# Two-layer hybrid decoder: wider weight ring, whole-row splits and five pair slots in the feed-forward parts

## The chip, the cores and the metric

The kernel runs on one core of one Trainium2 chip. A core has five engines with a queue each: TensorE (PE in the profile; its weight loads are a row of their own, PEld), VectorE (DVE), ScalarE (ACT), GpSimd (POOL) and SyncE (SP). On-chip memory is SBUF; matmuls accumulate in the banks of PSUM. The metric is the device time of one execution in microseconds, as the median of several runs. One of the executions is profiled, and its trace tells when each instruction ran.

## The reference

Two layers on a sequence of 256 tokens with 2048 features, all in float32. What matters here is the feed-forward part at the end of each layer, with w1 of 2048 x 8192 and w2 of 8192 x 2048:

```python
def squared_relu_mlp(h, w1, w2):
    z = jax.nn.relu(h @ w1)
    return (z * z) @ w2

for i in range(DEPTH):          # 2
    ...
    x = x + jnp.concatenate([token_out, mem_out], axis=-1) @ w_out[i]
    x = x + squared_relu_mlp(rms_norm(x, ffn_norm[i]), w_ff1[i], w_ff2[i])
```

The rest (a pooling mixer, two kinds of attention, projections) has weights of the same sort, which come through the same feed.

## The kernel before

**Splits.** A float32 operand goes into TensorE as two float32r parts: high = the value cast by ScalarE (`_split`, L179), low = value minus high, by VectorE (L182). A product takes three matmuls: high by high, low by high, high by low. So each weight is loaded, cast and subtracted before TensorE can use it. The class `Feed` does that for all weights in the order of use.

**Feed.** The host lays weights out as rows of 128 x 1024 in the order of use. There are two kinds of work on them. An N job (`quad`) uses 512 columns, half a plain row, as four blocks of 128 x 128. An S job belongs to a slab, two rows that hold a 2 x 2 arrangement of blocks of w2: by Strassen's scheme its seven products take sums of blocks as weights, and four S jobs serve them (j = 0 the first row, 1024 columns; 1 the sum `t1` of two blocks that a DMA accumulated, 512 columns; 2 the second row, 1024; 3 the first row again after VectorE has overwritten it with two sums, the step K, L205 and L207). A first pass of the program over dummies (`dry`) lists the jobs in a `Plan`; `close` makes the list of pieces to prepare.

**Ring.** The high and low parts lie in two rings, `hi_ring` and `lo_ring`, of SLOTS = 6 slots of 512 columns. `_slots` gives the next one or two neighbouring slots in turn, and goes back to the first where two don't fit before the end; where they are still in use the preparation stops and is tried again at the next job. `fill(job)` prepares pieces up to AHEAD = 3 places behind the job in the list; `free` gives a job's slots back. `load` issues the DMAs some loads further ahead (`loads_ahead`, 3, in most of the feed-forward part 4): plain rows and slab rows on SyncE's queue, the accumulating ones on GpSimd's. Four buffers hold plain rows (tile `raw`), three slab rows (tag `rows`, tile `slab`), and the second row of every second slab lies in a part of `room` (`feed.spare`).

The order of instructions on an engine is made by the framework from this program order and the data's dependencies; an instruction that is ready earlier may come ahead of one that stands before it in the program.

**Feed-forward part** (`ffn`, called once a layer). 64 tiles of 128 columns of w1 (`up_tile`), 16 blocks or four N jobs each, by `a_part` (L429 with the high parts for 512 columns, L431 with the low parts for 256), accumulate in one bank, `x_bank`. ScalarE copies the bank out (L812), VectorE adds its halves (L821), ScalarE squares (L827, L829). Two tiles make a pair: `convert` forms the sums that Strassen's scheme needs (L785 to L790), `high` casts them (L795) and `low` subtracts (L799) into one of six pair slots, four in `z` and two in `z_more` (tile `zb`). A pair's slot must be free (`pair_free`) before `high` is put in.

S jobs are put between the quads: `due` takes them from a list by a time, in tiles, that `tiles_at` gives each slab, at least two at the start of a tile, more after its fourth, eighth and twelfth block. Their matmuls are L865, L867 and L868 into seven banks `p`. The seven banks serve the left and the right half of the output in turns of four slabs: `swap` copies a bank to a kept buffer (L924) and the other half's sum back (L916), fourteen copies a turn. The buffers for that are `keep`: seven in `room` and two tiles of the tags `acc2` and `rowsq`. `close_left` sums the left half when it is done, `turn_left` transposes it; `evict` copies a bank into one of two buffers `outs`. Eight more tiles of w2 (`down_tile`, two N jobs each) end the part, between the last eight S jobs.

Of the kernel before, what the change touches and what calls it, by code (L numbers as in the profile page):

```python
# [17 lines left out]
P = 128  # L18
# [37 lines left out]
class Plan:  # L56
# [7 lines left out]
    def __init__(self):  # L64
        self.entries = []
        self.npos = 0
        self.jobs = []
        self.slabs = []

    def close(self):  # L70
        prep = []
        for job in self.jobs:

            prep.append(job)
            if job[0] == "S" and job[2] == 1:
                prep.append(("K", job[1]))
        self.prep = prep
        self.where = {job: i for i, job in enumerate(prep)}
        self.loads = []
        self.need = {}  # L80
        for p in prep:
            if p[0] == "S" and p[2] == 0:
                self.loads += [("S", p[1], 0), ("S", p[1], 1)]
            elif p[0] == "N" and p[1] % 2 == 0:
# [14 lines left out]
class Feed:  # L99


    def __init__(self, tc, wst, wpool, rows, plan, dry):
# [13 lines left out]
        if not dry:  # L116
            self.hi = wpool.tile([P, SLOTS * 512], F32R, name="hi_ring")
            self.lo = wpool.tile([P, SLOTS * 512], F32R, name="lo_ring")
            self.busy = [False] * SLOTS
            self.at = 0  # L120

# [43 lines left out]
    def _slots(self, n):  # L165
        a = self.at if self.at + n <= SLOTS else 0
        if any(self.busy[a : a + n]):
            return None
        for i in range(a, a + n):
            self.busy[i] = True  # L170
        self.at = (a + n) % SLOTS
        return a

    def _split(self, job, src, n):
        a = self._slots(n)
        if a is None:
            return False
        hi, lo = self.hi[:, a * 512 : (a + n) * 512], self.lo[:, a * 512 : (a + n) * 512]
# [9 lines left out]
        self.split[job] = (hi, lo, range(a, a + n))  # L188
        return True

    def _prepare(self, p):
        add = self.nc.vector.tensor_add
        self.load(self.plan.need[p] + 1 + self.loads_ahead)
        if p[0] == "N":
# [38 lines left out]
    def quad(self, what):  # L233

        job = ("N", self.pos // 4)
        if self.dry:
            self.plan.entries += what if isinstance(what, list) else [what]
            if self.pos % 4 == 0:
                self.plan.jobs.append(job)
            return Nothing(), Nothing()  # L240
# [24 lines left out]
    def job(self, n, j):  # L265
        job = ("S", n, j)
        if self.dry:
            self.plan.jobs.append(job)
            return Nothing(), Nothing()
# [18 lines left out]
def program(ctx, tc, plan, dry, xT, memT, par, lam, cst, wst, yT):  # L288
# [437 lines left out]
    def ffn(l, xs, tags, done):  # L726
# [9 lines left out]
        z_more = sp.tile([P, 2, 2, 1024], F32R, tag="big", name=f"zb{l}")  # L736
        staged = sp.tile([P, 2, 1024], F32, tag="big2", name=f"stage{l}")
        outs = [room[:, 512 * j : 512 * j + 512] for j in range(2)]
        feed.t1 = [room[:, 1024 + 512 * j : 1536 + 512 * j] for j in range(3)]
        two_y = room[:, 2560:3584].rearrange("p (a c) -> p a c", a=2)  # L740
        feed.spare = room[:, 3584:4608]
        keep = [room[:, 4608 + 512 * j : 5120 + 512 * j] for j in range(7)]
        for tag in ("acc2", "rowsq"):
            keep.append(tp.tile([P, 512], F32, tag=tag, bufs=1, name="keep"))
        r = []
        banks = []
        cnt = [0]
        done_pairs = set()
        pair_free = [True] * 6
        S1, S3, S2, S4, A12, A22, A11, A21 = range(8)  # L750

        def pair(i):
            i = i % 6
# [875 lines left out]
```

## Time and profile before

| | us |
|---|---|
| median of 3 runs | 2024.43 |
| lowest and highest run | 2023.85, 2027.73 |
| profiled execution | 2022.72 |
| its span | 2021.0 |

The granted TensorE clock was 1.0 throughout. The tiles 4 to 63 of the two feed-forward parts lie about 270 to 900 us and 1350 to 1985 us from the span's start. The loads:

```
raw<-in_w SPq DMA_DIRECT2D x484, 512.0 KB, 4.7
slab<-in_w SPq DMA_DIRECT2D x180, 512.0 KB, 5.3
room<-in_w POOLq DMA_DIRECT2D x180, 256.0 KB, 6.9
```

These are tile and source, queue, count, KB of each and the median us from issue to landing.

How to read the rest: a row of instructions has line, engine, operation, what is written and read (out<-in), shapes and count, then busy us and mean ns of one, then the engine's idle time before them and what ended it. A row of waits has the engine and tile that waited, whom it waited for, total us, times, longest us. Matmuls are pipelined: the one of 512 columns is listed with some 0.39 us, and the next begins 0.23 us after it. A wait shorter than the rest of the matmul before it shows no idle time of PE.

### The profile page before, as it was taken

What the parts mean: (1) busy time and instruction counts of PE and PEld (TensorE: products, weight loads), DVE (VectorE), ACT (ScalarE), POOL (GpSimd) and SP (SyncE); (2) the same over time, 40 slices, a digit from 0 to 9 for tenths busy, and PEclk for the clock granted to TensorE, in tenths of its full rate; (3) what the DMA queues carried; (4) which work ended last, traced back from release to release, by engine and by line L of the source; (5) the groups of instructions that cost most, each with busy time, mean ns of one, the idle gap of its engine ahead of it and who ended that gap; (6) DMA issues with size and microseconds to landing.
All of it is one profiled execution on the core that took longest, in us unless ns stands there. A gap on an engine that the chain in (4) does not pass through costs nothing.

```text
span 2021.0 us, 31924 instructions
## 1 busy us (share of the span) xinstructions
PE 2000.6 (99%) x10510; PEld 1694.8 (84%) x10510; DVE 1701.0 (84%) x2842; ACT 1486.9 (74%) x2582; POOL 260.5 (13%) x307
## 2 busy tenths in 40 slices
PE   9999999999999999999999999999999999999999
PEld 8888888888888888888888888888888888888887
DVE  8888878888888888989765698878888888888898
ACT  7765577687787878878665699567686877878875
POOL 0001211111111111110000000321111111111110
PEclk9999999999999999999999999999999999999999
DMA  8566588999999999975566534578899999999994
GB/s 320 168 204 189 189 252 242 284 266 281 276 271 288 273 266 275 265 231 176 184 233 194 171 126 149 196 211 262 261 274 269 282 278 279 272 283 272 269 275 142
DMA packets 162310, 485.11 MB, mean 240 GB/s; under 512 B 18272, under 2 KB 20960, under 8 KB 162144
## 3 DMA queue, kind: packets, MB, share of 16 engines
q1 hardware_dynamic: 127440, 420.14, 61.0%
q0 software_dynamic: 34560, 62.93, 18.4%
q8 instruction: 82, 1.34, 0.3%
q14 instruction: 84, 0.69, 0.1%
q10 hardware_dynamic: 144, 0.01, 0.0%
HBM read 480.91 MB, written 2.10 MB: 239 GB/s over the span
## 4 chain that ended last, share of the span: by engine, by line
PE 90%; ACT 5%; DVE 3%; issue 1%; DMA 1%; DVEq 0%; ACTq 0%; POOLq 0%
PE x_bank L429 20%; PE x_bank L431 10%; PE p L868 8%; PE p L865 8%; PE p L867 8%; PE wo L429 6%; PE wo L431 3%; ACT hi_ring L179 2%; PE u L429 2%; DVE lo_ring L182 1%; PE ff L429 1%; PE u L431 1%; PE q L463 1%; PE q L465 1%; PE q L464 1%
## 5 line engine op out<-in xcount | busy, mean ns | idle before, releaser
L179 ACT CAST hi_ring<-raw 128x512 fp32r<-128x512 f32 x969 | 590.9, 621 | 260.7 <-DVE lo_ring L182 58.9
L182 DVE TENSOR_TENSOR lo_ring<-raw,hi_ring 128x512 fp32r<-128x512 f32 x969 | 661.9, 697 | 114.9 <-ACT hi_ring L179 100.5
L429 PE MATMUL x_bank<-fx,hi_ring 128*128 128x512 f32 x1952 | 611.2, 394 | 1.2 <-ACT hi_ring L179 1.2
L182 DVE TENSOR_TENSOR lo_ring<-slab,hi_ring 128x1024 fp32r<-128x1024 f32 x300 | 365.5, 1223 | 123.8 <-ACT hi_ring L179 120.5
L431 PEld LDWEIGHTS x_bank<-fx,lo_ring 128*128 128x128 f32 x1952 | 365.8, 188 | 89.8 <-DVE lo_ring L182 6.9
L179 ACT CAST hi_ring<-slab 128x1024 fp32r<-128x1024 f32 x300 | 313.5, 1052 | 141.7 <-PE x_bank L429 64.8
L431 PE MATMUL x_bank<-fx,lo_ring 128*128 128x256 f32 x1952 | 384.6, 278 | 3.4 <-DVE lo_ring L182 3.4
L429 PEld LDWEIGHTS x_bank<-fx,hi_ring 128*128 128x128 f32 x1952 | 320.8, 189 | 28.9 <-ACT hi_ring L179 2.1
L865 PE MATMUL p<-hi_ring,z 128*128 128x512 f32 x588 | 231.8, 394 | 2.8 <-ACT hi_ring L179 2.5
L867 PE MATMUL p<-hi_ring,z 128*128 128x512 f32 x588 | 229.9, 391 | 0.0
L868 PE MATMUL p<-lo_ring,z 128*128 128x512 f32 x588 | 227.6, 393 | 0.4 <-DVE lo_ring L182 0.4
L154 POOL DMA_DIRECT2D room<-in_w x120 | 104.5, 876 | 580.3 <-DMA room<-in_w 564.6
L179 ACT CAST hi_ring<-room 128x512 fp32r<-128x512 f32 x180 | 137.7, 767 | 36.7 <-PE p L867 21.0
L429 PE MATMUL wo<-cat,hi_ring 128*128 128x512 f32 x512 | 161.8, 397 | 0.3 <-DVE rc L400 0.3
L182 DVE TENSOR_TENSOR lo_ring<-room,hi_ring 128x512 fp32r<-128x512 f32 x180 | 155.5, 864 | 6.6 <-ACT hi_ring L179 6.4
L144 POOL DMA_DIRECT2D slab<-in_w x60 | 51.9, 865 | 783.8 <-DVE mm_max L652 352.6
L868 PEld LDWEIGHTS p<-lo_ring,z 128*128 128x128 f32 x588 | 110.0, 188 | 29.6 <-DVE lo_ring L182 6.6
L865 PEld LDWEIGHTS p<-hi_ring,z 128*128 128x128 f32 x588 | 110.3, 188 | 20.4 <-ACT hi_ring L179 6.4
L867 PEld LDWEIGHTS p<-hi_ring,z 128*128 128x128 f32 x588 | 110.5, 188 | 13.7
L431 PEld LDWEIGHTS wo<-cat,lo_ring 128*128 128x128 f32 x512 | 95.9, 188 | 22.0
L868 PE MATMUL p<-lo_ring,zb 128*128 128x512 f32 x252 | 99.7, 396 | 2.0 <-DVE lo_ring L182 1.9
L431 PE MATMUL wo<-cat,lo_ring 128*128 128x256 f32 x512 | 101.5, 279 | 0.0
(382 smaller groups left out, 3270.8 us busy)
## 6 DMA issues: line engine op xcount, KB each, us to landing
raw<-in_w SPq DMA_DIRECT2D x484, 512.0 KB, 4.7
slab<-in_w SPq DMA_DIRECT2D x180, 512.0 KB, 5.3
room<-in_w POOLq DMA_DIRECT2D x180, 256.0 KB, 6.9
room<-in_w SPq DMA_DIRECT2D x120, 256.0 KB, 5.0
room<-in_w SPq DMA_DIRECT2D x60, 512.0 KB, 5.1
slab<-in_w POOLq DMA_DIRECT2D x60, 256.0 KB, 6.0
memraw<-in_mem SPq DMA_DIRECT2D x5, 512.0 KB, 4.2
resid<-in_x SPq DMA_DIRECT2D x8, 256.0 KB, 5.4
```

The costliest lines, as they stand in the source:

```text
L144: self.nc.gpsimd.dma_start(t[:, 0:512], self.wst[h, :, 512:1024], accum_op=ALU.add)
L154: self.nc.gpsimd.dma_start(self.t1[i], right, accum_op=ALU.add)
L179: self.last_cast = self.nc.scalar.copy(hi, src)
L182: low = self.nc.vector.tensor_sub(lo, src, hi.bitcast(F32))
L429: nc.tensor.matmul(ps, hi, xs[:, k, :], start=first and c == 0, stop=False)
L431: nc.tensor.matmul(ps[:, T : 2 * T], lo, xs[:, k, 0:T], start=False, stop=last and c == len(ks) - 1,)
L463: nc.tensor.matmul(ps[t], x[t][1], hi, start=k == 0, stop=False)
L464: nc.tensor.matmul(ps[t], x[t][0], hi, start=False, stop=False)
L465: nc.tensor.matmul(ps[t], x[t][0], lo, start=False, stop=k == NK - 1)
L865: nc.tensor.matmul(ps, a[1], hi, start=new, stop=False, **again)
L867: nc.tensor.matmul(ps, a[0], hi, start=False, stop=False, **again)
L868: nc.tensor.matmul(ps, a[0], lo, start=False, stop=end, **again)
```

## The change

`SLOTS` stays 6, and three more slots are used while a feed-forward part is on (`feed.more`): two in the half of `z_more` that the sixth pair slot had, for wide pieces, and one in two tiles of the tags `acc2` and `rowsq`, for the S job of 512 columns alone. `_slots` now takes any free place of the fitting size, beginning with the next, and pieces of two slots begin at even slots. In a feed-forward part a plain row's two N jobs are one piece, D: one cast and one subtraction over 1024 columns; its slots are given back one by one, as each quad is used, and `where` puts both quads at D's place in the list. Pair slots go from six to five. The two buffers `outs` are gone: `evict` and the last tiles go through the list `keep`, whose nine buffers all lie in `room`.

```diff
@@ -66,22 +66,29 @@
         self.npos = 0
         self.jobs = []
         self.slabs = []
+        self.wide = set()
 
     def close(self):
         prep = []
+        self.where = {}
         for job in self.jobs:
-
+            if job[0] == "N" and job[1] % 2 == 0 and {job, ("N", job[1] + 1)} <= self.wide:
+                self.where[job] = self.where["N", job[1] + 1] = len(prep)
+                prep.append(("D", job[1]))
+                continue
+            if job in self.where:
+                continue
+            self.where[job] = len(prep)
             prep.append(job)
             if job[0] == "S" and job[2] == 1:
                 prep.append(("K", job[1]))
         self.prep = prep
-        self.where = {job: i for i, job in enumerate(prep)}
         self.loads = []
         self.need = {}
         for p in prep:
             if p[0] == "S" and p[2] == 0:
                 self.loads += [("S", p[1], 0), ("S", p[1], 1)]
-            elif p[0] == "N" and p[1] % 2 == 0:
+            elif p[0] in "ND" and p[1] % 2 == 0:
                 self.loads.append(("N", p[1] // 2))
             self.need[p] = len(self.loads) - 1
         rows = sorted(self.loads, key=lambda r: r[0] == "N" and 8 * r[1] + 8 > self.npos)
@@ -116,8 +123,10 @@
         if not dry:
             self.hi = wpool.tile([P, SLOTS * 512], F32R, name="hi_ring")
             self.lo = wpool.tile([P, SLOTS * 512], F32R, name="lo_ring")
-            self.busy = [False] * SLOTS
+            self.busy = [False] * (SLOTS + 3)
             self.at = 0
+            self.more = None
+        self.in_ffn = False
 
     def load(self, upto):
         while self.lp < min(upto, len(self.plan.loads)):
@@ -162,20 +171,31 @@
             ),
         )
 
-    def _slots(self, n):
-        a = self.at if self.at + n <= SLOTS else 0
-        if any(self.busy[a : a + n]):
+    def _slots(self, job, n):
+        ext = job in self.plan.wide and self.more is not None
+        if job[0] == "S" and n == 1 and ext:
+            places = [SLOTS + 2]
+        else:
+            last = SLOTS + 2 if ext and n == 2 else SLOTS
+            first = (self.at + n - 1) // n * n
+            places = [(first + i) % last for i in range(0, last, n)]
+        free = [a for a in places if not any(self.busy[a : a + n])]
+        if not free:
             return None
+        a = free[0]
         for i in range(a, a + n):
             self.busy[i] = True
-        self.at = (a + n) % SLOTS
-        return a
+        if a < SLOTS + 2:
+            self.at = a + n
+        if a < SLOTS:
+            return range(a, a + n), [x[:, a * 512 : (a + n) * 512] for x in (self.hi, self.lo)]
+        return range(a, a + n), self.more[0] if n == 2 else self.more[1]
 
     def _split(self, job, src, n):
-        a = self._slots(n)
-        if a is None:
+        got = self._slots(job, n)
+        if got is None:
             return False
-        hi, lo = self.hi[:, a * 512 : (a + n) * 512], self.lo[:, a * 512 : (a + n) * 512]
+        slots, (hi, lo) = got
         self.last_cast = self.nc.scalar.copy(hi, src)
         if self.cast_behind:
             self.order(self.last_cast, self.cast_behind.pop())
@@ -185,12 +205,22 @@
         if self.behind:
             self.order(low, self.behind)
             self.behind = None
-        self.split[job] = (hi, lo, range(a, a + n))
+        self.split[job] = (hi, lo, slots)
         return True
 
     def _prepare(self, p):
         add = self.nc.vector.tensor_add
         self.load(self.plan.need[p] + 1 + self.loads_ahead)
+        if p[0] == "D":
+            r = ("N", p[1] // 2)
+            one, two = ("N", p[1]), ("N", p[1] + 1)
+            if not self._split(one, self.raw[r], 2):
+                return False
+            del self.raw[r]
+            hi, lo, (a, b) = self.split[one]
+            for job, s, c in ((one, a, 0), (two, b, 512)):
+                self.split[job] = (hi[:, c : c + 512], lo[:, c : c + 512], (s,))
+            return True
         if p[0] == "N":
             r = ("N", p[1] // 2)
             c = p[1] % 2 * 512
@@ -237,6 +267,8 @@
             self.plan.entries += what if isinstance(what, list) else [what]
             if self.pos % 4 == 0:
                 self.plan.jobs.append(job)
+                if self.in_ffn:
+                    self.plan.wide.add(job)
             return Nothing(), Nothing()
         if self.pos % 4 == 0:
             self.fill(job)
@@ -266,6 +298,7 @@
         job = ("S", n, j)
         if self.dry:
             self.plan.jobs.append(job)
+            self.plan.wide.add(job)
             return Nothing(), Nothing()
         self.fill(job)
         return self.split[job][:2]
@@ -734,24 +767,23 @@
         z = sp.tile([P, 4, 2, 1024], F32R, tag=tags[0], name=f"z{l}")
         room = sp.tile([P, 8192], F32, tag=tags[1], name=f"room{l}")
         z_more = sp.tile([P, 2, 2, 1024], F32R, tag="big", name=f"zb{l}")
+        one_more = [tp.tile([P, 512], F32R, tag=t, bufs=1, name="t1_" + t) for t in ("acc2", "rowsq")]
+        feed.more = ([z_more[:, 1, e, :] for e in range(2)], one_more)
+        feed.in_ffn = True
         staged = sp.tile([P, 2, 1024], F32, tag="big2", name=f"stage{l}")
-        outs = [room[:, 512 * j : 512 * j + 512] for j in range(2)]
-        feed.t1 = [room[:, 1024 + 512 * j : 1536 + 512 * j] for j in range(3)]
-        two_y = room[:, 2560:3584].rearrange("p (a c) -> p a c", a=2)
-        feed.spare = room[:, 3584:4608]
-        keep = [room[:, 4608 + 512 * j : 5120 + 512 * j] for j in range(7)]
-        for tag in ("acc2", "rowsq"):
-            keep.append(tp.tile([P, 512], F32, tag=tag, bufs=1, name="keep"))
+        feed.t1 = [room[:, 512 * j : 512 * j + 512] for j in range(3)]
+        two_y = room[:, 1536:2560].rearrange("p (a c) -> p a c", a=2)
+        feed.spare = room[:, 2560:3584]
+        keep = [room[:, 3584 + 512 * j : 4096 + 512 * j] for j in range(9)]
         r = []
         banks = []
-        cnt = [0]
         done_pairs = set()
-        pair_free = [True] * 6
+        pair_free = [True] * 5
         S1, S3, S2, S4, A12, A22, A11, A21 = range(8)
 
         def pair(i):
-            i = i % 6
-            return z[:, i] if i < 4 else z_more[:, i - 4]
+            i = i % 5
+            return z[:, i] if i < 4 else z_more[:, 0]
 
         class Chunks:
 
@@ -764,9 +796,13 @@
                     return half
                 return half[:, 0 if c.start == 0 else 1, :]
 
+        def free_tile():
+            x = keep.pop(0)
+            keep.append(x)
+            return x
+
         def evict(ps):
-            x = outs[cnt[0] % 2]
-            cnt[0] += 1
+            x = free_tile()
             nc.scalar.copy(x, ps)
             return x
 
@@ -788,10 +824,10 @@
                 )
                 nc.vector.tensor_sub(block(S2), block(S1), block(A11))
                 nc.vector.tensor_add(block(S4), block(A12), block(S2))
-                at(1, lambda: when(lambda: pair_free[i % 6], high))
+                at(1, lambda: when(lambda: pair_free[i % 5], high))
 
             def high():
-                pair_free[i % 6] = False
+                pair_free[i % 5] = False
                 nc.scalar.copy(pair(i)[:, 0, 0:n], u[:, 0:n])
                 at(1, low)
 
@@ -836,7 +872,7 @@
             assert all(k // 2 in done_pairs for k in ks)
             if n >= 3:
                 c_tile(ps, "w_ff2", l, n, ks, Chunks())
-                x = outs[cnt[0] % 2]
+                x = free_tile()
                 nc.vector.tensor_mul(x[:, 0:T], ps[:, 0:T], r[0])
                 nc.vector.tensor_add(resid[:, n, :], resid[:, n, :], x[:, 0:T])
                 done(n)
@@ -896,7 +932,7 @@
                     product(p, g, end, side(a), hi[:, s], lo[:, s])
                 feed.job_used(n, j)
                 if j == 3 and not again and i < 28:
-                    pair_free[i % 6] = True
+                    pair_free[i % 5] = True
 
             return run
 
@@ -1073,6 +1109,8 @@
                     tick()
                 if n == 2:
                     finish_banks()
+                if n == 7:
+                    feed.in_ffn, feed.more = False, None
                 down_tile(n, bank() if n < 3 else mmt("ff2"))
 
         return last
```

## The prediction

> **What bounds the kernel now.** First the page of the profile, its busy times:
>
> ```profile
> span 2021.0 us, 31924 instructions
> PE 2000.6 (99%) x10510; PEld 1694.8 (84%) x10510; DVE 1701.0 (84%) x2842; ACT 1486.9 (74%) x2582; POOL 260.5 (13%) x307
> ```
>
> TensorE is busy 99% of the span, so all that any change outside it can win are the moments in which it waits. The list of waits tells for whom (total us, times, longest). The tiles `x_bank` and `p` exist in the two feed-forward parts alone, so these rows are theirs:
>
> ```profile
> PEld p L868 <- DVE lo_ring L182: 14.6, 37, 1.0
> ...
> PEld p L865 <- ACT hi_ring L179: 8.9, 22, 0.8
> ...
> PE x_bank L431 <- DVE lo_ring L182: 3.4, 4, 1.3
> ...
> PE p L865 <- ACT hi_ring L179: 3.3, 8, 0.6
> ...
> PE x_bank L429 <- DVE z L799: 2.3, 2, 1.2
> PE p L868 <- DVE lo_ring L182: 2.3, 5, 0.6
> ...
> PE x_bank L429 <- ACT hi_ring L179: 1.2, 2, 0.6
> ```
>
> Four of the PE rows are waits for a weight piece whose high part (ScalarE, L179) or low part (VectorE, L182) was not ready: 3.4 + 3.3 + 2.3 + 1.2 = 10.2 us of idle TensorE in 19 waits. The one for L799 is the end of each part, where the last pair is converted; the diff doesn't touch that chain. The two PEld rows show that the weight loader waits more often, mostly under a running matmul.
>
> One such wait in the timeline (start, duration, engine, line):
>
> ```profile
> 415.04 0.59 ACT L924 COPY keep<-p 128x512 f32<-128x512 f32 x1
> ...
> 415.51 0.61 ACT L924 COPY room<-p 128x512 f32<-128x512 f32 x1
> ...
> 415.99 1.13 ACT L916 COPY p<-room 128x512 f32<-128x512 f32 x2
> ...
> 417.03 2.02 ACT L179 CAST hi_ring<-slab 128x1024 fp32r<-128x1024 f32 x2
> ...
> 418.13 2.36 DVE L182 TENSOR_TENSOR lo_ring<-slab,hi_ring 128x1024 fp32r<-128x1024 f32 x2 [2.17 <-ACT hi_ring L179]
> ...
> 418.37 0.40 PE L865 MATMUL p<-hi_ring,z 128*128 128x512 f32 x1
> 418.60 0.40 PE L867 MATMUL p<-hi_ring,z 128*128 128x512 f32 x1
> ...
> 419.41 0.50 PE L868 MATMUL p<-lo_ring,z 128*128 128x512 f32 x1 [0.41 <-DVE lo_ring L182]
> 419.74 0.40 PE L865 MATMUL p<-hi_ring,z 128*128 128x512 f32 x1
> ```
>
> ScalarE is exchanging the banks' sums (copies out, L924, and back, L916), so the cast of the slab begins at 417.03, its low part follows at 418.13, and TensorE, there at 418.60 and due on at 418.83, goes on at 419.41. What a wait costs is read here: the step 418.60 to 419.41 is 0.81 us where 418.37 to 418.60 is 0.23, so 0.58 are lost though the row says 0.41, and the next step (0.33) loses another 0.10. A wait costs its idle time plus 0.27 us.
>
> Outside these bursts ScalarE has time, and what holds it is the ring:
>
> ```profile
> ACT hi_ring L179 <- PE x_bank L429: 135.4, 179, 2.5
> ...
> ACT hi_ring L179 <- PE p L867: 73.0, 86, 2.5
> ...
> ACT hi_ring L179 <- DMA raw<-in_w: 6.8, 5, 2.4
> ```
>
> and on SyncE's queue:
>
> ```profile
> SPq L135 <- DVE lo_ring L182: 677.4, 384, 9.5
> ```
>
> 208.4 us it stands before a cast because TensorE has not yet let go of the slot, and 6.8 us for a load. The loads wait for buffers (677.4 us on SyncE's queue) and not buffers for loads. So the waits of TensorE come from too short a lead of the splits against bursts on ScalarE, and the lead is set by the slots.
>
> **The change part by part.**
>
> The order of the matmuls, their number and the DMAs (number and bytes) stay. Removed, added and moved are splits and buffers:
>
> *Rows split whole.* A plain row (1024 columns, two quads) has one cast and one subtraction in place of two each.
>
> ```profile
> L179 ACT CAST hi_ring<-raw 128x512 fp32r<-128x512 f32 x969 | 590.9, 621 | 260.7 <-DVE lo_ring L182 58.9
> L182 DVE TENSOR_TENSOR lo_ring<-raw,hi_ring 128x512 fp32r<-128x512 f32 x969 | 661.9, 697 | 114.9 <-ACT hi_ring L179 100.5
> ...
> L182 DVE TENSOR_TENSOR lo_ring<-slab,hi_ring 128x1024 fp32r<-128x1024 f32 x300 | 365.5, 1223 | 123.8 <-ACT hi_ring L179 120.5
> ...
> L179 ACT CAST hi_ring<-slab 128x1024 fp32r<-128x1024 f32 x300 | 313.5, 1052 | 141.7 <-PE x_bank L429 64.8
> ```
>
> The trace has the wide forms on slabs: 1052 ns for 2 x 621 and 1223 for 2 x 697. A part has 64 tiles of two rows and seven of the last eight tiles of one, 135 rows, 270 in both: ScalarE loses 270 x 190 ns = 51 us of work, VectorE 270 x 171 ns = 46 us. Off the path of TensorE: counted as 0 by itself. The price is latency: the first quad is whole after 1.05 + 1.22 = 2.27 us in place of 0.62 + 0.70 = 1.32, so 0.95 later if the cast begins at the same moment. The cover is the lead worked out below; without it, this is the second rival. A raw row is let go by one subtraction rather than the second of two, so its next load is not later; SyncE's order of issue is the order of the splits' loads as before.
>
> *Ring.* Before, six slots of 512 columns taken in turn, with waste at the wrap; a tile's usual order is S S N N S N S N (S a slab job, N a quad), 2+2+1+1+2+1+2+1 slots. After, four places of two slots, and a place of its own for the one narrow S job of four. The jobs' lengths, at a tile's start:
>
> ```profile
> 420.92 0.65 ACT L179 CAST hi_ring<-raw 128x512 fp32r<-128x512 f32 x1
> ...
> 421.82 0.40 PE L865 MATMUL p<-hi_ring,zb 128*128 128x512 f32 x1
> ...
> 422.02 0.59 ACT L812 COPY room<-x_bank 128x512 f32<-128x512 f32 x1
> ...
> 422.50 0.62 ACT L179 CAST hi_ring<-raw 128x512 fp32r<-128x512 f32 x1
> ...
> 423.19 0.39 PE L865 MATMUL p<-hi_ring,zb 128*128 128x512 f32 x1
> ...
> 423.87 0.61 PE L429 MATMUL x_bank<-fx,hi_ring 128*128 128x512 f32 x2
> ...
> 424.32 0.40 PE L431 MATMUL x_bank<-fx,lo_ring 128*128 128x256 f32 x2
> ...
> 425.25 0.63 PE L429 MATMUL x_bank<-fx,hi_ring 128*128 128x512 f32 x2
> ```
>
> A wide S takes 423.19 - 421.82 = 1.37 us, the narrow one 0.68, an N 425.25 - 423.87 = 1.38. Going through a part's order of jobs with the old rule and the new one, adding these lengths from the job that frees the slot to the job that uses it: before, some 4 of 10 wide S pieces have 2.75 us (one N, one S) or less, the median is 3.5, quads lie between 2.7 and 4.8. After, nearly all S pieces have 4.8 us or more (median 6.2), and rows 5 us or more, but for about 12 of 125 in a part that have 2.7. So the lead grows by some 2 us where it was shortest, and 0.95 of that goes into the latency of the rows; the slabs keep all of it. The waits to be covered are 0.1 to 1.3 us. What bounds it from both sides: nothing is won if the lead isn't used; and all 19 waits are won, 10.2 + 19 x 0.27 = 15.3 us, with perhaps 3 more from loader waits that delay a matmul by a tenth and show as no idle time (18). I take 12: two of the 19, the longest (1.3 us, one in each part, where the left half's banks are closed and VectorE sums them), come from VectorE's queue rather than from slots, and I leave them: 15.3 - 2 x (1.3 + 0.27) = 12.2.
>
> *Five pair slots.* Pair i is written about tile 2i + 3 and needs pair i-5 to be used up. By the slabs' due times the tightest are pairs 9 (pair 4 is free at tile 20.96, wanted at 21), 13 (28.6 against 29) and 5 (12.4 against 13). Nothing is delayed: 0. If one were, the copy L795 would wait on ScalarE for one job (1.4 us), casts queued behind it, and the pair itself is wanted by slabs several tiles later; with some six tight places in two parts at most 6 x 1.4 us of a lead of 5 us, so still 0 on TensorE.
>
> *Eviction buffers.* `evict` and the last tiles take from the nine kept buffers, all now in `room`. While sums are out, two are free, as many as before. No instruction more or less: 0, and the wait for an older reader is the same.
>
> **Sum.** The profiled execution took 2022.72 us, 1.7 around the span of 2021.0. 2022.7 - 12.2 = 2010.5. The median of the three runs, 2024.43, lies 1.7 above the profiled one, so the forecast for a median is 2024.4 - 12.2 = 2012.2, said as 2012.
>
> **The rivals.**
>
> *The three-ahead rule binds, not the slots.* A job still prepares only three pieces ahead, the sums of a slab (K) count as one, and a row counts as one though it serves two jobs, so its second quad prepares nothing. At the start of a tile a row is then put in only two S jobs (2.05 to 2.74 us) ahead. Against it: the cast at 420.92 is that of the quad first used at 423.87, put in only with the job that begins at 421.82, and yet it ran 0.9 us before that job, so the queues run ahead of where pieces are put in. If it binds in the bursts, about half of the waits stay: -6, 2018.
>
> *The whole row comes too late at each tile's start (slower).* If a row's cast stands behind the eviction of the tile before (L812), it can't begin before 422.50: 0.68 after the tile's start at 421.82, and the low part is there 0.68 + 1.05 + 1.22 = 2.95 after it. The first low matmul is due at 424.32, 2.50 after it, wherever one of the two opening S jobs is narrow. Stall 0.45 + 0.10; about 31 tiles of a part, 62 in all: 34 us, less the 12: 2024 + 22 = 2046. It decides from the point where the cast begins 0.25 us or more after the tile's start. For it: the place in which it is put in. Against: the row at 420.92, ahead of the eviction, and the longer lead of the slots. The Trainium skill, page "Perfetto Trace Analysis", section "Optimizing Scalar/DVE Operations", speaks for this rival: where Scalar and Vector aren't saturated but cause bubbles on other engines, breaking up instructions may let work be done sooner, and this part of the change does the opposite. Here they are at 74% and 84% of the span and do cause the bubbles, so by that rule the sum would be the 2046 of this rival, by the rows of the slots 2012.
>
> *Loads become the limit, or nothing changes.* Splits that run 2 us earlier want their rows 2 us earlier.
>
> ```profile
> 265.00:900.00 635.00, 629.47 (x3215) 528.60 (x3214) 546.41 (x761) 489.85 (x741) 99.42 (x116) 1.00 0.92 269
> ```
>
> The DMA share of 0.92 in this stretch (the last but one figure) speaks for it; the 677 us that raw loads wait for buffers, against 6.8 us that casts wait for loads, speaks against. Then the waits keep their length under another name: 2024.
>
> **How the numbers follow.** Forecast (all slot waits but the two closing ones) 60%, three-ahead rule 18%, loads or nothing 10%, late rows 12%. A measurement of this kernel can hardly tell less than 0.2%, 4 us. Faster: 60 and nearly all of the 18, less what falls within 4 us: 75%. Slower: 13%; the rest, 12%, the same. The range goes from 18 us won (2006, with one for the spread of runs: 2005) to the case of no change with its spread (2026); outside lie the late rows and little else. The likeliest case alone is 2008 to 2016.
>
> **What would show it.** Right: casts and subtractions of rows as 128x1024 at 1.05 and 1.22 us, some 270 of them and 540 fewer narrow ones; the four rows of waits of TensorE for `hi_ring` and `lo_ring` down from 10.2 us to 3 or less; ScalarE's waits for TensorE before casts still large; the two waits for L799 as they are. The three-ahead rule: half of those rows stays, at bursts of L916 and L924. Late rows: new waits of `x_bank` L431 for `lo_ring` in every second tile, 2 us after its start, with the eviction ahead of the cast. Loads: casts waiting for DMA instead of for TensorE. Wrong altogether would be a span over 2030, or one that falls while the four rows stay.

## The result, and the profile after

| | before | after |
|---|---|---|
| median of 20 runs each | 2022.9 | 2028.4 |
| lowest, highest | 2020.1, 2027.7 | 2023.1, 2038.1 |
| profiled execution | 2022.72 | 2034.17 |

The time after is 1.0027 of the time before (95% interval 1.0019 to 1.0035): 5.5 us slower, where 12 us faster was forecast. The profiled execution of after lies 5.8 us above its median; its trace shows what kinds of loss there are, and their sizes hold for that execution.

The page of after, its span and busy times:

```profile
span 2032.4 us, 30761 instructions
...
PE 2006.1 (99%) x10510; PEld 1698.3 (84%) x10510; DVE 1690.6 (83%) x2574; ACT 1459.1 (72%) x2314; POOL 261.9 (13%) x307
```

TensorE executes as many instructions as before. VectorE and ScalarE have 268 fewer each, but the time that this frees is smaller than forecast: 10 us on VectorE (46 was said) and 28 on ScalarE (51). Two narrow casts that follow each other overlap: one row of the trace of before has such a pair at 1.13 us, where 2 x 0.62 was counted, and the wide cast takes 1.05. Likewise two narrow subtractions in a row take 1.29 (at 831.93 in before), where 2 x 0.70 was counted, and the wide one takes 1.22.

```profile
905.77 1.13 ACT L179 CAST hi_ring<-raw 128x512 fp32r<-128x512 f32 x2
```

The waits of TensorE after (total us, times, longest). L901 to L904 are the old L865 to L868, L462 and L464 the old L429 and L431, L835 the old L799, L848 and L806 the copies of a bank (old L812 and L770), `ff` the bank of a part's first three tiles:

```profile
PE x_bank L462 <- DVE z L835: 6.4, 2, 3.2
PE x_bank L462 <- ACT room L848: 3.3, 3, 2.3
PE p L904 <- DVE lo_ring L202: 2.3, 5, 0.5
PE p L901 <- DVE z L835: 1.6, 2, 0.8
...
PE x_bank L462 <- ACT room L806: 1.3, 2, 0.7
PE ff L462 <- ACT hi_ring L199: 1.2, 2, 0.6
PE ff L464 <- DVE lo_ring L202: 1.1, 2, 0.5
PE p L901 <- ACT hi_ring L199: 0.9, 4, 0.3
```

The waits that the change was to win did go: the four rows for `hi_ring` and `lo_ring` had 10.2 us in 19 waits, and 2.3 + 0.9 = 3.2 us in 9 are left. No wait of `x_bank` L464 for a low part is among them. What stands there instead is new, in three places.

**A part's start.** ScalarE after:

```profile
255.22 1.05 ACT L199 CAST hi_ring<-raw 128x1024 fp32r<-128x1024 f32 x1 [1.32 <-issue]
264.91 0.62 ACT L199 CAST t_acc<-room 128x512 fp32r<-128x512 f32 x1 [8.64 <-DMA room<-in_w]
265.44 0.58 ACT L848 COPY room<-ff 128x512 f32<-128x512 f32 x1
```

`t_acc` is the place of its own for the narrow S piece. Nobody holds that place at a part's start, so the piece's cast is put in at once, long before its accumulated row has landed. It stands at the head of ScalarE's queue for 8.64 us, and behind it stand the copy of the first bank and the casts of the first rows. TensorE pays in the `ff` rows and the one for L901 and L835: 1.2 + 1.1 + 1.6 = 3.9 us in six waits.

**A bank's copy.** ScalarE and TensorE around 1778 us, and one load on GpSimd's queue, after:

```profile
1770.84 0.86 POOL L153 DMA_DIRECT2D slab<-in_w  x1 [9.23 <-DMA raw<-in_w]
...
1773.66 1.05 ACT L199 CAST zb<-slab 128x1024 fp32r<-128x1024 f32 x1 [0.33 <-PE x_bank L462]
...
1776.21 0.39 PE L464 MATMUL x_bank<-fx,lo_ring 128*128 128x256 f32 x2
...
1778.04 0.39 PE L903 MATMUL p<-t_acc,z 128*128 128x512 f32 x1
...
1778.54 1.04 ACT L199 CAST hi_ring<-slab 128x1024 fp32r<-128x1024 f32 x1 [3.83 <-PE p L903]
1779.49 0.93 ACT L831 CAST z<-stage 128x896 fp32r<-128x896 f32 x1
...
1780.33 0.58 ACT L848 COPY room<-x_bank 128x512 f32<-128x512 f32 x1
...
1780.96 0.73 PE L462 MATMUL x_bank<-fx,hi_ring 128*128 128x512 f32 x2 [2.31 <-ACT room L848]
```

The tile's bank is full at 1776.6, and ScalarE has been idle since 1774.7. But the head of its queue is the cast of a slab's second row, and the accumulating load that completes this row (L153, issued at 1770.84) lands only at 1778.38; ScalarE passes its wait for that landing at 1778.40 and casts at 1778.54. The row names L903 as what ended the wait, because a matmul of it ended at 1778.43; but that one reads `t_acc`, the narrow place, and not a ring slot. So it is a late load, not a taken slot. Behind the cast stand a pair's high part (L831) and then the copy, and by then TensorE has nothing left to do without the bank. These rows were not there before; now L848 and L806 have 4.6 us in five waits. In all five ScalarE had first stood before such a cast, which began within 0.2 us of the landing of its accumulating load, though three of the five rows name TensorE.

**A part's end.** VectorE while the last pair is converted, after (L857 adds the halves, L821 to L826 form the sums, L835 is the low part that TensorE waits for; ScalarE's copy of the tile began at 895.60):

```profile
895.60 0.58 ACT L848 COPY room<-x_bank 128x512 f32<-128x512 f32 x1
...
895.73 1.23 DVE L202 TENSOR_TENSOR lo_ring<-slab,hi_ring 128x1024 fp32r<-128x1024 f32 x1 [1.22 <-ACT hi_ring L199]
...
897.47 0.69 DVE L857 TENSOR_TENSOR room<-room 128x512 f32<-128x512 f32 x1
...
899.93 1.23 DVE L202 TENSOR_TENSOR lo_ring<-slab,hi_ring 128x1024 fp32r<-128x1024 f32 x1 [1.17 <-ACT hi_ring L199]
901.07 0.42 DVE L821 TENSOR_TENSOR stage<-stage 128x256 f32<-128x256 f32 x1
901.41 1.22 DVE L202 TENSOR_TENSOR lo_ring<-raw,hi_ring 128x1024 fp32r<-128x1024 f32 x1
...
902.74 1.23 DVE L202 TENSOR_TENSOR lo_ring<-slab,hi_ring 128x1024 fp32r<-128x1024 f32 x1
903.88 0.29 DVE L826 TENSOR_TENSOR stage<-stage 128x128 f32<-128x128 f32 x1
...
905.28 1.23 DVE L202 TENSOR_TENSOR zb<-raw,zb 128x1024 fp32r<-128x1024 f32 x1
906.42 1.23 DVE L835 TENSOR_TENSOR z<-stage,z 128x1024 fp32r<-128x1024 f32 x1
```

Each short step stands behind a split of a piece that is needed later. The next instruction starts at 907.55, so the chain from the copy's start takes 907.55 - 895.60 = 11.95 us. Before, it began at 897.73 and ended like this:

```profile
897.73 0.58 ACT L812 COPY room<-x_bank 128x512 f32<-128x512 f32 x1
...
904.13 0.29 DVE L790 TENSOR_TENSOR stage<-stage 128x128 f32<-128x128 f32 x1
904.33 1.22 DVE L182 TENSOR_TENSOR lo_ring<-slab,hi_ring 128x1024 fp32r<-128x1024 f32 x1
905.46 0.69 DVE L182 TENSOR_TENSOR lo_ring<-room,hi_ring 128x512 fp32r<-128x512 f32 x1
906.07 1.22 DVE L799 TENSOR_TENSOR z<-stage,z 128x1024 fp32r<-128x1024 f32 x1
907.20 0.69 DVE L205 TENSOR_TENSOR slab<-room 128x512 f32<-128x512 f32 x1
```

That is 907.20 - 897.73 = 9.47 us. Of the 2.48 us more, 1.06 lie in the two stretches in which a row's whole split of 1.22 us stands (L821 to L826 and L826 to L835), and 1.42 ahead of them, where slab splits and sums stand. The wait at the end grew from 1.17 to 3.19 us, in both parts alike.

**The clock.** TensorE right behind that wait, after:

```profile
907.70 0.74 PE L462 MATMUL x_bank<-z,hi_ring 128*128 128x512 f32 x2 [3.19 <-DVE z L835]
...
908.84 0.63 PE L903 MATMUL p<-hi_ring,z 128*128 128x512 f32 x1
909.26 0.63 PE L904 MATMUL p<-lo_ring,z 128*128 128x512 f32 x1
...
911.82 0.50 PE L904 MATMUL p<-t_rowsq,z 128*128 128x512 f32 x1
```

From start to start a matmul of 512 columns takes 909.26 - 908.84 = 0.42 us in place of 0.23. In this trace the granted clock is 0.5 for 3.413 us from 908.6, from 1782.4 and from 2000.9, each time behind one of the long waits (3.19, 2.31 and 3.20 us). Half the clock for 3.41 us costs 1.7 us.

The sum of these, for the profiled executions: the ring waits give 7.0 us of idle time and ten times 0.27, -9.7; the start +3.9 and six times 0.27, +5.5; the banks' copies +4.6 and five times 0.27, +6.0; the ends 6.4 - 2.3, +4.1; the clock 3 x 1.7, +5.1. Together +11.0, where 2034.17 - 2022.72 = 11.45 was measured.

### The profile page after: what moved, and what is told of

It is laid out like the page before. It is cut to its first block, busy times and chain, and to the rows that moved or that the text cites. A ratio compares the mean times of both kernels' runs of the same rounds, so it can differ in the third digit from the quotient of the medians.

```text
span 2032.4 us, 30761 instructions
## 1 busy us (share of the span) xinstructions
PE 2006.1 (99%) x10510; PEld 1698.3 (84%) x10510; DVE 1690.6 (83%) x2574; ACT 1459.1 (72%) x2314; POOL 261.9 (13%) x307
## 4 chain that ended last, share of the span: by engine, by line
PE 85%; DVE 5%; DMA 4%; ACT 3%; issue 2%; ACTq 0%; DVEq 0%; SPq 0%; POOLq 0%
PE x_bank L462 19%; PE x_bank L464 9%; PE p L904 8%; PE p L901 8%; PE p L903 8%; PE wo L462 6%; PE wo L464 3%; DMA room<-in_w 3%; DVE lo_ring L202 2%; PE u L462 2%; DMA slab<-in_w 1%; ACT hi_ring L199 1%; PE u L464 1%; PE q L496 1%; PE q L498 1%
## 5 line engine op out<-in xcount | busy, mean ns | idle before, releaser
L202 DVE TENSOR_TENSOR lo_ring<-raw,hi_ring 128x512 fp32r<-128x512 f32 (+1 forms) x629 | 541.7, 869 | 139.8 <-ACT hi_ring L199 129.4
L199 ACT CAST hi_ring<-raw 128x512 fp32r<-128x512 f32 (+1 forms) x629 | 472.1, 755 | 258.9 <-DVE lo_ring L202 57.5
L462 PE MATMUL x_bank<-fx,hi_ring 128*128 128x512 f32 x1428 | 448.1, 395 | 3.2 <-ACT room L848 2.5
L464 PEld LDWEIGHTS x_bank<-fx,lo_ring 128*128 128x128 f32 x1428 | 268.8, 188 | 61.3
L464 PE MATMUL x_bank<-fx,lo_ring 128*128 128x256 f32 x1428 | 281.4, 278 | 0.0
L462 PEld LDWEIGHTS x_bank<-fx,hi_ring 128*128 128x128 f32 x1428 | 235.1, 189 | 25.7 <-ACT room L848 5.1
L901 PE MATMUL p<-hi_ring,z 128*128 128x512 f32 x446 | 176.2, 395 | 2.2 <-DVE z L835 1.6
L904 PE MATMUL p<-lo_ring,z 128*128 128x512 f32 x446 | 173.9, 397 | 2.5 <-DVE lo_ring L202 2.3
L903 PE MATMUL p<-hi_ring,z 128*128 128x512 f32 x446 | 175.3, 393 | 0.0
L462 PE MATMUL x_bank<-fx,zb 128*128 128x512 f32 x524 | 164.4, 395 | 1.5 <-ACT room L848 0.8
L462 PE MATMUL wo<-cat,hi_ring 128*128 128x512 f32 x512 | 161.7, 397 | 0.3 <-DVE rc L433 0.3
L153 POOL DMA_DIRECT2D slab<-in_w x60 | 51.9, 866 | 851.1 <-DVE osb L1525 361.9
L202 DVE TENSOR_TENSOR zb<-slab,zb 128x1024 fp32r<-128x1024 f32 x79 | 96.7, 1224 | 27.9 <-ACT zb L199 25.4
L464 PEld LDWEIGHTS x_bank<-fx,zb 128*128 128x128 f32 x524 | 98.4, 188 | 22.5
L464 PEld LDWEIGHTS wo<-cat,lo_ring 128*128 128x128 f32 x512 | 95.9, 188 | 22.0
L904 PEld LDWEIGHTS p<-lo_ring,z 128*128 128x128 f32 x446 | 83.4, 189 | 28.0 <-DVE lo_ring L202 10.9
L464 PE MATMUL x_bank<-fx,zb 128*128 128x256 f32 x524 | 103.2, 278 | 0.0
```

What stands on the lines that cost most here:

```text
L153: self.nc.gpsimd.dma_start(t[:, 0:512], self.wst[h, :, 512:1024], accum_op=ALU.add)
L199: self.last_cast = self.nc.scalar.copy(hi, src)
L202: low = self.nc.vector.tensor_sub(lo, src, hi.bitcast(F32))
L462: nc.tensor.matmul(ps, hi, xs[:, k, :], start=first and c == 0, stop=False)
L464: nc.tensor.matmul(ps[:, T : 2 * T], lo, xs[:, k, 0:T], start=False, stop=last and c == len(ks) - 1,)
L901: nc.tensor.matmul(ps, a[1], hi, start=new, stop=False, **again)
```

## The experiments

The theory after this reading: the wider ring wins what was forecast, and loses it again by a cast put in too early and by two waits at the parts' ends with the half clock behind them. The rivals: whole rows as such are too late; the losses are only idle time and the clock doesn't matter; a full TensorE queue at the ends helps any kernel, and the ring has no part in it. Each kernel differs from after unless said, and each ratio is to the kernel before, run beside it (medians 2022.8, 2023.8 and 2023.2 in the three groups).

**The narrow piece's cast held back** (the cast is ordered behind the cast put in before it; nothing else):

```diff
         slots, (hi, lo) = got
+        before = self.last_cast if job[0] == "S" and n == 1 else None
         self.last_cast = self.nc.scalar.copy(hi, src)
+        if before is not None:
+            self.order(self.last_cast, before.ins.name)
```

> The changed kernel, with the cast of the narrow piece held behind the cast of the piece before it in ScalarE's queue. Theory (an early cast blocks the queue): in the changed kernel the first narrow cast of a part stands on ScalarE for 8.6 us until its load lands, and TensorE waits three times at the part's start (0.59, 0.53, 0.80 us idle, with 0.27 each some 2.7 us a part). Held, these waits fall below 0.5 us in all and the time by 4 to 5 us against the changed kernel; the waits of 3.2 us at the parts' ends stay. Rival (rows split whole are too late at a part's start): no difference, the first waits stay as they are.

2021.13 us (11 runs), ratio 0.9995 (0.9984 to 1.0006): 7.3 us below after (6.5 by the two ratios), more than the 4 to 5 expected. Its waits of TensorE:

```profile
PE x_bank L465 <- DVE z L838: 6.0, 2, 3.1
PE p L907 <- DVE lo_ring L205: 1.9, 5, 0.7
PE tc_x L533 <- DVE acc L749: 1.4, 1, 1.4
```

The waits at the start are gone, and so are those for L851, the copy of a bank; of L809, the other copy, one of 0.6 us is left. The ends stay as they were, and so does the clock behind them: of the four windows of half clock in this trace one stands behind the first end, two behind the second, and one behind the wait of 1.36 us for L533.

**The narrow piece in a place of two slots, none of its own:**

```diff
         if job[0] == "S" and n == 1 and ext:
-            places = [SLOTS + 2]
-        else:
+            n = 2
+        if True:
```

> The changed kernel without the narrow place: the narrow piece takes a place of two slots of the ring. Theory (an early cast blocks the queue): the 8.6 us at a part's start are gone as with the held cast, but the lead of the other pieces shrinks, so that of the waits for slots that the change took away 2 to 5 us come back; in all 0 to 3 us faster than the changed kernel. Rival (rows too late): no better at the start, and slower in the body, 2 to 5 us slower than the changed kernel.

2023.58 us (11 runs), ratio 1.0001 (0.9991 to 1.0011). The start's waits are gone here too, by another way, so it is the early cast that makes them. It is 4.8 us below after, where 0 to 3 were expected. The waits for high parts have 4.2 us in five; but the longest, 2.9 us, is not for a slot: ScalarE stands 3.48 us before the cast of a slab (at 854.17) until its load has landed. The ends have their 3.2 each.

**The last pair's chain put in at once**, without the steps' delays by a job:

```diff
+                if i == 31:
+                    assert pair_free[i % 5]
+                    high()
+                    return
                 at(1, lambda: when(lambda: pair_free[i % 5], high))
```

(likewise for `low`, `square` and `convert` of that pair)

> The changed kernel, with the last pair's chain (add, squares, sums, high, low) put into the queues at once after the last tile, ahead of the splits for the last eight slab jobs and rows. Theory (the chain's steps each stand behind a split of 1.05 or 1.22 us): the wait of 3.2 us for the last pair's low part falls to 1.3 us or less in each part, the clock stays at 1.0 there, and the time falls by 2 x (1.9 + 1.7), some 7 us, against the changed kernel. Rival (the chain waits for data, not for its place): the wait stays within 0.5 us of 3.2 and the time the same.

2029.94 us (5 runs), ratio 1.0033 (1.0021 to 1.0045), and the two waits are 3.19 and 3.18 us: a miss, and what the rival had said. Where the steps stand in the program doesn't by itself set their order on VectorE: in this trace too L821 (902.25), L825 (903.72), L826 (905.06) and L842 (907.60, the old L835) each run right behind a split of 1.22 us. That each becomes ready only while a split is running or has just been taken is argued, not shown.

**Zero matmuls at the ends** (three matmuls of 512 columns that add zeros to the open bank, ahead of the last pair's blocks in each part):

```diff
+            if n == 0:
+                between = lambda b: idle(ps) if b == 6 else None
...
+        def idle(ps):
+            for _ in range(3):
+                nc.tensor.matmul(ps, zero[:, 0:P], zero, start=False, stop=False)
...
+        zero = keep.pop(0)
+        nc.vector.memset(zero, 0.0)
```

> The changed kernel with three matmuls of zero weights by zeros (float32, 512 columns) added into the open bank before the last pair's blocks, in each part: they add nothing to the sum and fill some 2.6 us of the wait of 3.2. Theory (an idle TensorE of 2 to 3 us brings the half clock for 3.4 us after it): the halves of the clock at the two ends are gone, the mean clock goes from 0.998 to 1.0 and the time falls by 2 x 1.7 = 3.4 us. Rival (the clock falls for another reason, or the half clock costs nothing because TensorE is ahead there): the clock or the time stays.

2027.66 us (12 runs, 2019.4 to 2037.4), ratio 1.0023 (1.0010 to 1.0036): by the median nothing is won. In the profiled execution the end waits are down to 0.60 and 0.63 and there is no half clock until the last matmul has ended, but the start's waits are there in part and the banks' copies cost as much as in after (3.1 us for L848, 1.8 for L806). The other executions have mean clocks of 0.997 to 1.0, so the half clock isn't gone from all of them. Alone it settles little.

**Both: the narrow cast held back and the zero matmuls.**

> The narrow cast held and the three matmuls of zeros before the last pair's blocks, together. If the half clock after the waits at the parts' ends costs time, this is 3 to 5 us faster than the narrow cast held alone (2021.1): some 2017, with a mean clock of 0.999 to 1.0. If the half clock is hidden behind the other engines there, 2021.

2011.59 us (5 runs, 2010.5 to 2011.7), ratio 0.9941 (0.9929 to 0.9953), faster than both kernels by 11 us and more, and 9.5 us below the held cast alone, where 3 to 5 were expected. The waits of TensorE that are left:

```profile
PE warm L406 <- PEq L1652: 0.8, 1, 0.8
PE tc_x L533 <- DVE acc L749: 0.7, 1, 0.7
PE p L913 <- DVE lo_ring L205: 0.5, 1, 0.5
PE p L910 <- ACT hi_ring L200: 0.5, 1, 0.5
```

The stretch around the first part's end, with the narrow cast held back alone and with the matmuls too (the granted clock is the figure after POOL's):

```profile
900.00:960.00 60.00, 56.21 (x307) 48.74 (x308) 54.88 (x111) 45.66 (x95) 0.00 (x0) 0.94 0.47 150
```

```profile
900.00:960.00 60.00, 59.16 (x329) 50.32 (x328) 58.56 (x120) 48.73 (x102) 0.00 (x0) 1.00 0.50 161
```

Against the kernel with the held cast alone, TensorE's idle time, added up over the whole trace, is 4.5 us in place of 13.1; six zero matmuls of 0.9 us add 5.4; four windows of half clock at 1.7 us are gone, one of them that behind L533, whose wait is 0.7 us here: -8.6 + 5.4 - 6.8 = -10.0, where the two profiled executions differ by 10.07 (2020.74 and 2010.67). The idle time alone would have given 3.2. The matmuls also changed an order. With the held cast alone a split of 1.22 us ran ahead of the last step (L838):

```profile
900.01 1.22 DVE L205 TENSOR_TENSOR zb<-raw,zb 128x1024 fp32r<-128x1024 f32 x1
901.15 1.22 DVE L838 TENSOR_TENSOR z<-stage,z 128x1024 fp32r<-128x1024 f32 x1
```

With the matmuls L838 runs at 900.17 and that split behind it, at 901.91.

**One zero matmul in place of three:**

```diff
-            for _ in range(3):
+            for _ in range(1):
```

> The narrow piece's cast held back as before, but one zero matmul in place of three at each part's end. Theory (the waits of 3 us at the two ends cost more than their idle time because the clock falls to half behind them, and a wait of 2 us still does that): end waits of about 2.1 us, windows of half clock after them, median 2015 to 2020. Rival (a wait costs its idle time alone): 3.6 us of zero matmuls less and 4.2 us of idle time more than with three of them, which took 2011.6: 2012, clock 0.999 to 1.0.

2010.98 us (5 runs), ratio 0.9938 (0.9926 to 0.9950), as fast. The expectation took the end waits for 2.1 us; they are 1.16 and 0.76, since the order changed as with three. So it doesn't try a wait of 2 us, and doesn't tell the two theories of it apart. It does show that waits of this size bring no half clock: none is in its trace before the last matmuls.

**The kernel before with the three zero matmuls:**

> The kernel before with the three zero matmuls ahead of the last pair's blocks in each part (the output is the reference's, the matmuls add zeros). Theory (the change's ring and whole rows are what the fast version lives on; the kernel before has no wait at a part's end that brings the clock down): six matmuls of 0.9 us add 5.4 us, the two end waits of 1.17 with their 0.27 go, 2.9 us, and the ring waits of the body stay: 2023.5 + 2.5 = about 2026, ratio 1.000 to 1.003. Rival (the filler alone made the gain, and the old ring with the filler does as well): 2011 to 2016, ratio under 0.997.

2024.01 us (12 runs), ratio 1.0007 (0.9998 to 1.0016): where the theory had 2026 and 1.000 to 1.003. The end waits are gone, and the ring waits of the old kernel are nearly all there, 9.2 of 10.2 us:

```profile
PE x_bank L431 <- DVE lo_ring L182: 3.4, 4, 1.3
PE p L871 <- ACT hi_ring L179: 3.2, 9, 0.6
...
PE p L874 <- DVE lo_ring L182: 1.4, 4, 0.6
...
PE x_bank L429 <- ACT hi_ring L179: 1.2, 2, 0.6
```

The rival that the matmuls make the gain by themselves falls. With them the old ring takes 2024 and the new one, with the narrow cast held back, 2011.6.

**Rows in halves again**, with the eight slots of the changed ring (a half row may take any of them) and the cast held back:

```diff
-            if job[0] == "N" and job[1] % 2 == 0 and {job, ("N", job[1] + 1)} <= self.wide:
-                self.where[job] = self.where["N", job[1] + 1] = len(prep)
-                prep.append(("D", job[1]))
-                continue
```

> The narrow cast held, and plain rows split in two halves as before the change, each half in one of eight slots; so of the change there remain the slots, the pair slots and the buffers. If rows split whole are too late (0.95 us more latency), the waits of TensorE for raw pieces fall and the wait at the parts' ends shrinks by about a microsecond, 2 to 4 us faster than with rows whole (2021.1). If latency doesn't matter in the body because the lead is long, 2020 to 2022, with the end the same. If whole rows help by relieving ScalarE and VectorE, 2 us or more slower.

2040.16 us (6 runs), ratio 1.0079 (1.0063 to 1.0095), 19 us above the same kernel with whole rows.

```profile
PE x_bank L464 <- ACT room L850: 21.8, 15, 3.5
...
ACT hi_ring L199 <- DMA raw<-in_w: 39.8, 20, 4.4
```

TensorE waits for bank copies (L850) fifteen times, and ScalarE stands before casts of rows that haven't landed; ahead of nine of the fifteen late copies stands a row's cast that has just waited for its load. It is the picture of 1778 us again: more slots let casts be put in earlier than their source is there, and what stands behind them is late. In this ring, then, rows split whole are no loss but a gain of 19 us. How is argued, not shown: half rows may be cast earlier, and they may take odd slots, which leaves fewer pairs of slots for the slabs; the two aren't told apart. Whole rows with the old ring of six slots were not tried.

**Only the last eight tiles' rows in halves**, cast held back:

```diff
         def last():
+            feed.in_ffn = False
             for n in range(8):
```

> The narrow cast held, and only the rows of the last eight tiles split in halves. The last pair's chain stands behind a 1.22 us subtraction of a row just before its low part, and a 1.04 us cast before its high part. If these set the wait at the end, it falls from 3.0 to about 2.0 to 2.4 us in each part, 1 to 3 us faster than 2021.1; if the slab splits ahead in the chain set it, the wait stays at 3.

2018.95 us (12 runs), ratio 0.9974 (0.9963 to 0.9984). The end waits are 1.25 and 2.65 in place of 3.09 and 2.93, and the only half clock before the kernel's end stands behind the 2.65. The time is 2.2 us below that with all rows whole, as expected, but by its interval this may be next to nothing; the end waits are not the 2.0 to 2.4 us of the expectation. A row's whole split in the chain is thus part of the wait at the ends and not all of it.

## Why the prediction was wrong

**The term for the ring was right.** Forecast were 15.3 us of loss in 19 waits, 12.2 of them won. After has 9.7 less by the same count; where nothing else spoils it, the kernel with both edits against the one before, the profiled executions differ by 2022.72 - 2010.67 = 12.05, with 5.4 us of zero matmuls in it. The sum by the prediction's price of a wait: idle time 16.6 to 4.5 us, -12.1; 21 waits of the parts (the 19 and the two ends) down to 3, 18 x 0.27, -4.9; the matmuls +5.4: -11.6. That also bears out the price of idle time plus 0.27. It even won the two waits of 1.3 us that I had left to VectorE's queue: no trace with the new ring has that row, though two of them (the last pair's chain put in at once, and the zero matmuls alone) have one of 1.2 and 1.3 us for a high part near the same places.

**The steps that failed.** Two things were put at nothing, and the sum above has their price: the casts that stand in ScalarE's queue before their loads have landed (5.5 us at the parts' starts, 6.0 at the banks' copies, 1.7 of half clock), and the last pair's chain (4.1 us at the ends, 3.4 of half clock behind them).

**"The one for L799 is the end of each part [...] the diff doesn't touch that chain".** The diff leaves the chain's instructions alone, but they run on VectorE and ScalarE between splits, and the splits are what it changes. The chain went from 9.47 to 11.95 us and the wait from 1.17 to 3.19. The prediction put whole rows at 0 with the lead of the ring as cover. That cover is TensorE's, for the pieces; the chain at the end has none.

**"A place of its own", and the longer lead, were counted only as a gain.** What an earlier cast does to the queue it stands in was not asked: a free slot lets the narrow cast be put in before its load is there, and ScalarE's queue waits with it. The prediction said that "the queues run ahead of where pieces are put in" and took it for a comfort. The slabs' casts at the banks' copies are the same case. Against it the prediction set that "the loads wait for buffers [...] and not buffers for loads"; that was read from the kernel before, and with the longer lead it no longer held for every cast. The rows of ScalarE's casts that wait for loads had 6.8 us for plain rows and 2.8 for slabs before, 9.6 in all; after they have 49.5, and 24.7 with the narrow cast held back. The narrow casts alone have

```profile
ACT t_acc L199 <- DMA room<-in_w: 17.3, 2, 8.7
```

**No term for the clock.** The granted clock was 1.0 throughout the trace of before, so a wait was priced at its idle time plus 0.27. That holds for waits up to 1.3 us; those near 3 us at the ends cost 1.7 or more on top.

**The rivals.** The three-ahead rule: not borne out, 3.2 of 10.2 us were left and not half. Late rows at each tile's start: no such wait came, and halves were slower; the mechanism that a whole row delays what stands behind it was right, its place was not the tile's start but the part's end. Loads or nothing: in part. Its sign, casts that wait for DMA, came (9.6 to 49.5 us), but not by the DMA engines as a limit of the whole: the loads are late for single casts, at the head of ScalarE's queue, and the kernel with both edits gained its 11 us with 26.3 us of such waits left. Five pair slots and the kept buffers: no wait for a pair slot or for a buffer shows, counted as 0 and never tried apart.

**What is open.** Why the waits for L851 went with the held cast: that one cast's place changed the order of others is argued, not shown, and in the kernel with one zero matmul one of them is back (1.8 us, behind a slab's cast that waited for its accumulating load). Why the zero matmuls move the last split behind L838, likewise. How after's runs come to spread over 15 us, where those of the two fastest kernels lie within 1.2 and 3.3, was not followed run by run; which waits reach the half clock is one candidate.

## What to carry to other kernels

A deeper ring does not only give the consumer lead: it lets producers' instructions be put in before their data is there, and on ScalarE here each of them held up whatever stood behind it (8.64 us at a part's start, 3.83 at a bank's copy). So for each queue list the short urgent steps (a bank's copy, the last conversion before a drain) and ask what may now stand ahead of them. When a wait's row names an engine that was itself idle, look at the head of that engine's queue and at what it waits for, loads included. A wait of TensorE near 2 us or more is worth filling or splitting first, ahead of many short ones, since the clock can make it dearer than its length.

## What the hardware showed that was not expected

The half clock came for waits well below the length of its own window. In the traces of these eleven kernels all stretches of half clock begin on a grid of 3.413 us within a trace (the three in after are 256 and 64 such windows apart) and last one or two windows. Cutting each trace along its grid and adding up TensorE's idle time in every window gives, for the window that follows (those already at half clock left out, and the end of the kernel):

| idle in a window, us | windows | followed by half clock |
|---|---|---|
| 0.8 to 1.3 | 34 | 0 |
| 1.3 to 1.7 | 9 | 1 |
| 1.7 to 1.9 | 6 | 2 |
| over 1.9 | 13 | 13 |

So 1.9 us of idle time in a window, a little over half of it, was always enough, and where a wait falls on the grid decides: one of 1.79 us that lay across a boundary brought nothing, in the kernel with one zero matmul, and neither did the longest of all, 3.47 us with rows in halves, which a boundary cut into 1.87 and 1.59. The Trainium skill, page "TensorE: Matmul & The Clock Gate", section "What's actually happening", has the window: 3413 ns and free-running. The trace agrees on both. The same section lets the clock fall after at least one idle window of about 3.4 us; here 1.9 us of idle time in a window was enough every time.
